# A hybrid attention and linear-attention block: the attention stage issued in the source's order on every engine

## The chip, the cores and the metric

The kernel runs on one core of one Trainium2 chip. A core has a matrix engine (TensorE, PE in the profile), a vector engine (VectorE, DVE), an engine for activation functions and copies (ScalarE, ACT), GpSimd (POOL) and SyncE (SP), which here only issues transfers. Each takes its own instructions in the order in which they were put, and waits for the others through semaphores. The metric is the time of one execution in microseconds of device time (us), the median of a few runs.

## The reference, cut to what matters

One layer on 512 tokens of width 2048, all in float32. A row norm with a scale and a shift gives `h`. One projection of `h` feeds two mixers: 16 heads of attention of width 64, and 4 heads of a gated linear attention (GLA). Both are gated, joined, projected out and added to the input. What the change touches is the attention:

```python
aq, ak, av, ag, gq, gk, gv, gg, lr_f, lr_b = split(h @ w_in)
for window, dilation in ((128, 1), (512, 4), (2048, 16)):
    o_p, lse_p = dilated_window_attention(aq, ak, av, rel_bias, window, dilation)
mix_w = softmax(stack(lses))
att = einsum('pbsh,pbshe->bshe', mix_w, stack(outs))
a_out = att * silu(ag)
```

The kernel computes the three patterns as one softmax per head over all 512 keys: a row of biases for each head holds the relative bias plus the logarithm of how many patterns contain a distance, and a very large penalty where none does.

## The kernel before

**Precision.** TensorE multiplies in a reduced format. So each operand is split into a high part (an ACT copy, for weights `split_hi`, L313) and a low part (a DVE subtraction, `split_lo`, L297), and every product is three matmuls (`three`, L168 to L171).

**Units.** The projections are cut into units of 512 output columns: `qk2`, `qk4`, `qk6` (queries and keys of two pairs of heads each), `gk`, `gv0`, `gv1`, `ag0` to `gg1`, and the output projection. A unit (`unit`, L843) has 8 weight groups of 512 KB. For each group it runs four output tiles, two depth blocks each, three matmuls per block. I call such a block of three matmuls a **tick**: 64 ticks to a unit. The four tiles accumulate in four of five PSUM banks (`PJ`); the unit that follows starts in the bank that is free and then in those of the one before, so these must have been copied out.

**Copying out.** `qk_evict` (L531) copies the queries and keys of a pair out of two banks and splits them. It has four ACT copies of 64 partitions (L539, L548), four DVE subtractions (L540, L550) and four small transfers through SP (L549, L551), which put keys on the other half of the partitions.

**Attention beside the projections.** While one unit multiplies, the attention of the two pairs that the unit before produced runs between its ticks. `attention` (L556) makes 16 tiles (4 heads, 4 blocks of 128 queries), each of these steps:

- `score`: two matmuls (L576, L577) into one of three other banks (`PA`). DVE then adds the bias and takes the row's minimum (L580, here "the reduction"), ACT takes the exponential (L583), DVE the reciprocal of the sum (L584), and POOL scales P (L585).
- `turn`: four TensorE transposes of P into a `PA` bank (L597), a high part by ACT (L601) and a low part by DVE (L602).
- `values`: for two tiles together, eight matmuls into a `PA` bank (L611), an ACT copy (L614) and a DVE addition (L618).

The list `items` says at which share of the unit each step is put (`ATT_AT`, L73). What lies past the unit's end goes into `spill` and is put into the next unit.

**Sums.** Two matrix-vector products (the value bias and the gate of the end) are done by DVE in 48 pieces (`sum_work`, L686), each with a load of 512 KB. `SUMS_IN` (L78) says how many pieces ride in which unit.

**Order.** TensorE's order is that of the source throughout (L145). On the other engines the planner of the first stage sets the order up to L518; from there on a scheduler lists the instructions by their priority, and `urgent` (L837) raises the steps of the attention by 20 places. So an early step of a later unit can come ahead of a late one. All loads of weights go through SP (L286), four buffers deep (`RAW`).

Of the kernel before, what the change touches and what calls it, by code (L numbers as in the profile page):

```python
# [18 lines left out]
P = 128  # L19
# [114 lines left out]
def block_kernel(ctx: ExitStack, tc: tile.TileContext, a: dict):  # L134
# [396 lines left out]
    def qk_evict(p, psq, psk):  # L531

        for j in range(2):
            own = slice(64 * j, 64 * j + 64)
            oth = slice(64 - 64 * j, 128 - 64 * j)
            qs = T2(f"qs{p}{j}", F32R)
            act(qs[own], psq[own, ::-1], AF.Copy, scale=-0.125)  # L539
            stt(qs[oth], psq[own, ::-1], -0.125, qs[own].bitcast(F32),  # L540
                op0=ALU.mult, op1=ALU.subtract)
            stacks[2 * p + j] = [qs, None, None, own]
        for j in range(2):
            own = slice(64 * j, 64 * j + 64)
            oth = slice(64 - 64 * j, 128 - 64 * j)
            ks = T2(f"ks{p}{j}", F32R)
            kl = T2(f"kl{p}{j}", F32R)
            act(ks[own], psk[own], AF.Copy)  # L548
            nc.sync.dma_start(ks[oth].bitcast(F32), ks[own].bitcast(F32))  # L549
            tt(kl[own], psk[own], ks[own].bitcast(F32), op=ALU.subtract)  # L550
            nc.sync.dma_start(kl[oth].bitcast(F32), kl[own].bitcast(F32))  # L551
            stacks[2 * p + j][1:3] = ks, kl

    cat = [None] * 4

    def attention(pairs):  # L556

        tiles = [(2 * p + j, i) for p in pairs for j in range(2) for i in range(4)]
        gt, pt, pr_ = {}, {}, {}
        heads = [2 * p + j for p in pairs for j in range(2)]  # L560

        def g_load(h):
            g = gp.tile([P, 896], F32, tag="g", name=f"g{h}")
            nc.sync.dma_start(g, bass.AP(grow.tensor, grow.offset + h * 1024, [[1, P], [1, 896]]))
            gt[h] = g

        def score(h, i):
            def go():
                if h % 8 == 0 and i == 0:
                    cat[h // 8] = B8(f"cat{h // 8}", [4, 512])  # L570
# [5 lines left out]
                mm(ps, qs[:, q], ks, start=True, stop=False)  # L576
                mm(ps, qs[:, q], kl, start=False, stop=True)  # L577
                t = T2(f"p{h}{i}")
                st = sm.tile([P, 3], F32, tag="st", name=f"st{h}{i}", bufs=6)
                nc.vector.tensor_tensor_reduce(  # L580
                    out=t, in0=ps, in1=gt[h][:, P * i:P * i + 512], op0=ALU.add, op1=ALU.min,
                    scale=1.0, scalar=3e38, accum_out=st[:, 0:1])
                act(t, t, AF.Exp, bias=st[:, 0:1], scale=-1.0, accum_out=st[:, 1:2])  # L583
                nc.vector.reciprocal(st[:, 2:3], st[:, 1:2])  # L584
                nc.gpsimd.tensor_scalar(t, t, st[:, 2:3], 1.0, op0=ALU.mult, op1=ALU.mult)  # L585
                pr_[h, i] = t
            return go

        def turn(h, i):
            def go():  # L590
                half, ii = divmod(i, 2)
                if ii == 0:
                    pt[h, half] = B8(f"pt{h}{half}", [2, 4, 256], F32R)
                t = pr_.pop((h, i))
                pk = PA(f"t{h}{i}")
                for kt in range(4):
                    nc.tensor.transpose(pk[:, kt * P:kt * P + P], t[:, kt * P:kt * P + P], ident)  # L597
                hi = pt[h, half][:, 0, :, P * ii:P * ii + P]
                lo = pt[h, half][:, 1, :, P * ii:P * ii + P]
                src = pk.rearrange("p (k q) -> p k q", k=4)  # L600
                act(hi, src, AF.Copy)  # L601
                tt(lo, src, hi.bitcast(F32), op=ALU.subtract)  # L602
            return go

        def values(h, half):
            def go():
                t = pt.pop((h, half))
                po = PA(f"o{h}{half}")
                for kt in range(4):
# [10 lines left out]

        items = []
        n = len(tiles)
        for x in range(n + 4):
            if x < n:
                items.append(score(*tiles[x]))
            if 2 <= x <= n + 1:
                items.append(turn(*tiles[x - 2]))
            if 3 <= x <= n + 2 and tiles[x - 3][1] % 2 == 1:
                items.append(values(tiles[x - 3][0], tiles[x - 3][1] // 2))
        g_load(heads[0])  # L630
        start, span, move0, move1, move_last = ATT_AT
        at = [start + (q + 0.5) / len(items) * span for q in range(len(items))]
        at[0] -= move0
        at[1] -= move1
        at[-1] += move_last
        return list(zip(at, items))

    def gate_half(m, z):

# [203 lines left out]
    def unit(name, natural, side=(), rhs=None, lr=None, tiles=range(4)):  # L843
# [5 lines left out]
        for q in range(KT // 2):  # L849
            g = gorder[q] if name == "o3" else q  # L850
            i0 = gi[name, g]
            todo = []
            if 0 in tiles:
                todo = list(range(gi[name, gorder[0] if name == "o3" else 0], upto[name, g] + 1))
                for i in todo:
                    split_hi(i)
                for ahead in (1, 2):
                    fetch(upto[name, g] + ahead)
            if i0 not in low:
                split_lo(i0)  # L860
            hi, lo = wts[i0]
            for n, i in enumerate(tiles):
                for kk in range(2):
                    k = 2 * g + kk
                    rh, rl = (h_hi[:, k, :], h_lo[:, k, :]) if rhs is None else rhs[k]
                    if natural:
                        t = slice(i * P, i * P + P)
                        cw = slice(kk * 512, kk * 512 + 512)
                        three(ps[n], rh[:, t], rl[:, t], hi[:, cw], lo[:, cw], q + kk == 0, q + kk == KT // 2)
                    else:  # L870
                        c = slice(kk * 512 + i * P, kk * 512 + i * P + P)
                        three(ps[n], hi[:, c], lo[:, c], rh, rl, q + kk == 0, q + kk == KT // 2)
                    tick += 1
                    if tick % (2 * len(tiles)) == 2:
                        for i_ in todo:
                            split_lo(i_)
                    while pos < len(side) and side[pos][0] * ticks <= tick:
                        urgent(side[pos][1])
                        pos += 1
                if lr is not None:  # L880
                    lr(4 * g + i)
            for i_ in todo:
                split_lo(i_)
        while pos < len(side):
# [12 lines left out]
        lnexp()  # L897


    for p in range(2):  # L900
        qk_evict(p, psb["b", 4 + 2 * p], psb["b", 5 + 2 * p])
    for n, p in (("qk2", 0), ("qk4", 2), ("qk6", 4)):
        ps = unit(n, False, attention((p, p + 1)) + ([(0.05, shift_row)] + some_sums(n) if p == 4 else []))
        for q in range(2):
            qk_evict(p + 2 + q, ps[2 * q], ps[2 * q + 1])

    ps = unit("gk", False, attention((6, 7)) + some_sums("gk"))
    gla["k"] = B8("gkt", [4, 512])
    for i in range(4):
        act(gla["k"][:, i, :], ps[i], AF.Copy)  # L910


    lrb = B8("lrb", [KT, 32])
    nc.sync.dma_start(lrb, a["w_lr"][0])
    lrs = B8("lrs", [KT, 2, 32], F32R)
    act(lrs[:, :, 0, :], lrb, AF.Copy)
    tt(lrs[:, :, 1, :], lrb, lrs[:, :, 0, :].bitcast(F32), op=ALU.subtract)
    plr = PA("plr")

    def lr_tick(n):  # L920
        if n % 2 == 1:
            k = n // 2
            w = lrs[:, k, :, :].rearrange("p a b -> p (a b)")
            mm(plr[:64], w, h_hi[:, k, :], start=k == 0, stop=False)
            mm(plr[:64], w, h_lo[:, k, :], start=False, stop=k == KT - 1)

    ps = unit("gv0", True, some_sums("gv0"), lr=lr_tick)
    gla["v0"] = B8("gv0", [4, 512])
    for i in range(4):
        act(gla["v0"][:, i, :], ps[i], AF.Copy)  # L930
# [200 lines left out]
```

## Time and profile before

| what | us |
|---|---|
| runs: median (lowest to highest of 3) | 962.89 (958.9 to 962.98) |
| the profiled execution, its own time | 959.9 |
| its span, first to last instruction | 957.9 |
| first matmul of `qk2` / `qk4` / `qk6` / `gk` / `gv0` | 191.87 / 257.29 / 323.71 / 390.28 / 457.51 |
| mean granted TensorE clock (1 is full speed) | 0.997 |

The stage that the change orders anew runs from the first matmul of `qk2` to that of `gv1` at 510.39 us. A row of the timeline has start, length, engine, line, operation, output and inputs, count, and in brackets the idle time ahead of it with what ended it. Matmuls overlap: what one costs is the distance from its start to the next start, not its length. "SPq" and "ACTq" are the issues of transfers by these engines.

### The profile page before, as it was taken

To read this page: it belongs to the slowest core of one execution; us is meant where nothing else is said; L and a number is where in the kernel's file an instruction comes from. 1 tells how busy PE (TensorE), PEld (TensorE's weight loads), DVE (VectorE), ACT (ScalarE), POOL (GpSimd) and SP (SyncE) were. 2 spreads that over 40 slices of the span, in tenths; PEclk is the share of its full clock that TensorE was granted. 3 is DMA by queue.
4 is the path that set the end of the run, shared out by engine and by line. 5 is a ranking of instruction groups with operands and counts; after the bars stand their busy time and mean duration, and the time that the engine had idled before them with its cause. 6 is when DMAs were issued, how large, how long until landed. Compare 5 with 4: busy or idle time off the path is not lost.

```text
span 957.9 us, 11999 instructions
## 1 busy us (share of the span) xinstructions
PE 939.7 (98%) x4464; PEld 777.1 (81%) x4464; DVE 605.3 (63%) x900; ACT 431.5 (45%) x719; POOL 81.1 (8%) x100
## 2 busy tenths in 40 slices
PE   8999999999999999999999999999999999999996
PEld 5888788888888888888778888888887888888884
DVE  7988899675756676766435656675964352546421
ACT  5443533565655655655215544543834152233222
POOL 0000000012122022122000000000010000202120
PEclk9999999999999999999999999999999999999998
DMA  9999687443333463533454244354555464244013
GB/s 330 413 411 365 229 296 275 150 131 105 112 103 105 144 200 108 173 127 103 150 176 146 86 132 154 132 176 154 173 195 183 132 221 154 92 151 152 23 55 121
DMA packets 45180, 163.76 MB, mean 171 GB/s; under 512 B 5730, under 2 KB 6018, under 8 KB 40386
## 3 DMA queue, kind: packets, MB, share of 16 engines
q1 hardware_dynamic: 44946, 162.68, 49.9%
q8 instruction: 35, 0.57, 0.2%
q10 hardware_dynamic: 176, 0.33, 0.1%
q14 instruction: 23, 0.18, 0.1%
HBM read 154.51 MB, written 4.28 MB: 166 GB/s over the span
## 4 chain that ended last, share of the span: by engine, by line
PE 84%; DMA 6%; DVE 5%; issue 3%; ACT 1%; SPq 0%; POOL 0%; ACTq 0%; DVEq 0%; POOLq 0%
PE ps_o L170 6%; PE ps_o L169 6%; PE ps_o L171 6%; DMA rawg<-in_wg 6%; PE ps_qk L170 5%; PE ps_qk L169 5%; PE ps_qk L171 5%; PE o L611 3%; PE sta L169 3%; PE sta L170 3%; PE sta L171 3%; PE stb L171 3%; PE stb L169 3%; PE stb L170 3%; PE ps_gv L171 3%; PE ps_gv L170 3%
## 5 line engine op out<-in xcount | busy, mean ns | idle before, releaser
L585 POOL TENSOR_SCALAR p<-p,st 128x512 f32<-128x512 f32 x64 | 45.5, 711 | 406.6 <-DVE st L584 357.9
L244 DVE CUSTOM_DVE_ANT_0 cb<-cb,sb,c_bcond 128x2048 f32<-128x2048 f32 (+1 forms) x32 | 73.4, 2294 | 0.0
L583 ACT ACTIVATE p<-p,st 128x512 f32<-128x512 f32 x64 | 46.1, 721 | 56.8 <-DVE st L580 56.3
L602 DVE TENSOR_TENSOR pt<-t,pt 128x512 fp32r<-128x512 f32 x64 | 44.0, 689 | 16.2 <-ACT pt L601 15.8
L580 DVE CUSTOM_DVE_ANT_0 p<-s,g 128x512 f32<-128x512 f32 x64 | 43.6, 687 | 14.8 <-PE s L577 14.5
L601 ACT ACTIVATE pt<-t 128x512 fp32r<-128x512 f32 x64 | 37.8, 592 | 10.2 <-PE t L597 9.2
L244 DVE CUSTOM_DVE_ANT_0 rawg<-rawg,sb,gate 128x1024 f32<-128x1024 f32 x16 | 20.5, 1283 | 29.6 <-DMA rawg<-in_wg 29.6
L611 PEld LDWEIGHTS o<-pt,vv 128*128 128x128 f32 x256 | 34.7, 188 | 5.0 <-DVE pt L602 2.2
L597 PEld LDWEIGHTS t<-c_ident,p 128*128 128x128 f32 x256 | 31.8, 140 | 8.5
L597 PE MATMUL t<-c_ident,p 128*128 128x128 f32 x256 | 38.3, 272 | 0.0
L611 PE MATMUL o<-pt,vv 128*128 128x256 f32 x256 | 36.6, 283 | 0.9 <-DVE pt L602 0.8
L244 DVE CUSTOM_DVE_ANT_0 rawg<-rawg,sb,c_bcond 128x1024 f32<-128x1024 f32 x16 | 20.5, 1283 | 26.3 <-DMA rawg<-in_wg 26.3
L1014 POOL TENSOR_TENSOR x<-x,fgain 128x512 f32<-128x512 f32 x12 | 20.3, 1696 | 185.3 <-ACT ysq L1012 185.3
L1012 ACT ACTIVATE ysq<-x 128x512 f32<-128x512 f32 x16 | 10.1, 632 | 47.2 <-DVE x L1010 47.2
L767 POOL TENSOR_SCALAR dc<-st,sc 128x256 f32<-128x256 f32 x16 | 10.4, 652 | 245.5 <-DVE st L764 240.6
L1009 DVE TENSOR_TENSOR y<-ps_o,sb 128x512 f32<-128x512 f32 x16 | 10.9, 684 | 25.9 <-PE ps_o L171 25.9
L584 DVE RECIPROCAL st<-st 128x1 f32<-128x1 f32 x64 | 10.3, 162 | 24.9 <-ACT p L583 24.9
L576 PE MATMUL s<-ks,qs 128*128 128x512 f32 x64 | 25.1, 391 | 0.0
L577 PE MATMUL s<-kl,qs 128*128 128x512 f32 x64 | 25.0, 391 | 0.0
L774 ACT ACTIVATE sq<-st,sc 128x256 f32<-128x256 f32 x24 | 12.2, 509 | 26.8 <-DVE st L769 14.3
L1010 DVE TENSOR_TENSOR x<-y,x 128x512 f32<-128x512 f32 x16 | 18.0, 1125 | 0.3
L614 ACT ACTIVATE oh<-o 64x256 f32<-64x256 f32 x32 | 12.2, 382 | 13.0 <-PE o L611 12.2
(1275 smaller groups left out, 2916.7 us busy)
## 6 DMA issues: line engine op xcount, KB each, us to landing
cb<-in_wm SPq DMA_DIRECT2D x31, 1024.0 KB, 7.9
rawg<-in_wg SPq DMA_DIRECT2D x32, 512.0 KB, 3.4
raw_o<-in_w_o SPq DMA_DIRECT2D x32, 512.0 KB, 3.4
raw_qk<-in_w_qk SPq DMA_DIRECT2D x24, 512.0 KB, 3.4
rawb<-in_w_sb SPq DMA_DIRECT2D x16, 512.0 KB, 4.8
rawv<-in_wv SPq DMA_DIRECT2D x16, 512.0 KB, 3.8
raw_gv<-in_w_gv SPq DMA_DIRECT2D x16, 512.0 KB, 3.5
raw_ag<-in_w_ag SPq DMA_DIRECT2D x16, 512.0 KB, 3.3
```

What stands on the lines that cost most here:

```text
L169: mm(ps, lh, rh, start=first, stop=False)
L170: mm(ps, ll, rh, start=False, stop=False)
L171: mm(ps, lh, rl, start=False, stop=last)
L244: nc.vector.tensor_tensor_reduce(out=w, in0=w, in1=with_, op0=ALU.mult, op1=ALU.add, scale=1.0, scalar=init, accum_out=dst)
L576: mm(ps, qs[:, q], ks, start=True, stop=False)
L580: nc.vector.tensor_tensor_reduce(out=t, in0=ps, in1=gt[h][:, P * i:P * i + 512], op0=ALU.add, op1=ALU.min, scale=1.0, scalar=3e38, accum_o ...
L583: act(t, t, AF.Exp, bias=st[:, 0:1], scale=-1.0, accum_out=st[:, 1:2])
L585: nc.gpsimd.tensor_scalar(t, t, st[:, 2:3], 1.0, op0=ALU.mult, op1=ALU.mult)
L597: nc.tensor.transpose(pk[:, kt * P:kt * P + P], t[:, kt * P:kt * P + P], ident)
L601: act(hi, src, AF.Copy)
L602: tt(lo, src, hi.bitcast(F32), op=ALU.subtract)
L611: mm(po[:, :256], vv[h // 4][:, kt, h % 4, :], t[:, w, kt, :], start=kt == 0 and w == 0, stop=kt == 3 and w == 1)
```

## The change

From the copying out of the first pairs to the end of `gv0`, POOL, DVE, ACT and SP now take the source's order too. With it:

- `attention` puts the end of the `score` step (reciprocal and scaling) into a step of its own, `scale`. It lies 0.75 tiles behind the score, and for the last tile ahead of the unit's end. The turn lies 1.8 tiles behind the score, the values 3.2, and a tile takes 0.057 of a unit from a start at 0.12. The last turns and values fall into the next unit.
- `qk_evict` does query and key of one half together.
- The units `qk4`, `qk6` and `gk` begin with a double step: each output tile takes weight groups 0 and 1 before the next tile starts, so the second bank is wanted after 4 ticks instead of 2. The unit ahead splits both groups; the second one's low part comes after its last tick.
- Loads of `qk` and `gk` weights (from the fourth on) and of bias tiles are issued by ACT instead of SP.
- `qk6` and `gk` carry no sums; `gv0` has 12 pieces instead of 9, `gv1` 5 instead of 2, `ag0` 8 instead of 7, `gg1` 5 instead of 4.
- The small weights `lrb` and their splits, wanted in `gv0`, are loaded and split inside `gk`.
- A second way to transpose P (DVE and a trip through memory) is written, but `BY_DVE = ()` leaves it unused: TensorE transposes all of P as before.

```diff
-ATT_AT = (0.17, 0.8, 0.04, 0.05, 0.05)
+ATT_AT = (0.12, 0.057)
+BY_DVE = ()
-SUMS_IN = {"qk6": 4, "gk": 4, "gv0": 9, "gv1": 2, "ag0": 7, "ag1": 9, "gg0": 9}
+SUMS_IN = {"gv0": 12, "gv1": 5, "ag0": 8, "ag1": 9, "gg0": 9}
...
-            nc.sync.dma_start(raws[i], a["w_" + u][g])
+            queue = nc.scalar if u[:2] in ("qk", "gk") and i > 2 else nc.sync
+            queue.dma_start(raws[i], a["w_" + u][g])
...
+            qs, ks, kl = [T2(f"{n}{p}{j}", F32R) for n in ("qs", "ks", "kl")]
             act(qs[own], psq[own, ::-1], AF.Copy, scale=-0.125)
+            act(ks[own], psk[own], AF.Copy)
             stt(qs[oth], psq[own, ::-1], -0.125, qs[own].bitcast(F32),
                 op0=ALU.mult, op1=ALU.subtract)
...
             tt(kl[own], psk[own], ks[own].bitcast(F32), op=ALU.subtract)
-            nc.sync.dma_start(kl[oth].bitcast(F32), kl[own].bitcast(F32))
-            stacks[2 * p + j][1:3] = ks, kl
+            for t in (ks, kl):
+                nc.sync.dma_start(t[oth].bitcast(F32), t[own].bitcast(F32))
+            stacks[2 * p + j] = [qs, ks, kl, own]
...
+        for x in range(n):
+            h, i = tiles[x]
+            items.append((x, score(h, i)))
+            items.append((min(x + 0.75, n - 0.6), scale(h, i)))
+            half, ii = divmod(i, 2)
...
+                items.append((x + 1.8, pe_turn(h, i)))
+                if ii:
+                    items.append((x + 3.2, values(h, half)))
...
+        start, step = ATT_AT
+        return [(start + step * x, go) for x, go in items]
...
+        steps = [order_[:2]] if name in ("qk4", "qk6", "gk") else [order_[:1], order_[1:2]]
+        for step in steps + [[g] for g in order_[2:]]:
             todo = []
             if 0 in tiles:
+                end = upto[name, step[-1]] + (name[:2] == "qk" and step[-1] == order_[-1])
...
+                        if len(step) == 2 and tick == 8:
+                            split_hi(end)
+                            for ahead in (1, 2):
+                                fetch(end + ahead)
+                        if tick == 10 if len(step) == 2 else tick % (2 * len(tiles)) == 2:
+                            for i_ in todo:
+                                if i_ <= upto[name, step[-1]]:
+                                    split_lo(i_)
...
+    with tc.manual_schedule(engines=PLANNED):
+        side = attention((0, 1))
+        for i in range(3):
+            fetch(i)
+        split(0)
+        for p in range(2):
+            qk_evict(p, psb["b", 4 + 2 * p], psb["b", 5 + 2 * p])
+        for n, p in (("qk2", 0), ("qk4", 2), ("qk6", 4)):
+            ps = unit(n, False, side + ([(0.6, shift_row)] if p == 4 else []))
+            side = attention((p + 2, p + 3))
+            for q in range(2):
+                qk_evict(p + 2 + q, ps[2 * q], ps[2 * q + 1])
...
+        ps = unit("gk", False, side + [(0.7, lr_load), (0.85, lambda: lr_part(0)), (0.9, lambda: lr_part(1))])
...
+        ps = unit("gv0", True, some_sums("gv0"), lr=lr_tick)
```

More of the change, by code (lines that the diff above doesn't have):

```diff
@@ L587, in score, with pe_turn @@
             return go
-        def turn(h, i):
+        def pe_turn(h, i):
             def go():
@@ L597, in go @@
                     nc.tensor.transpose(pk[:, kt * P:kt * P + P], t[:, kt * P:kt * P + P], ident)
-                hi = pt[h, half][:, 0, :, P * ii:P * ii + P]
-                lo = pt[h, half][:, 1, :, P * ii:P * ii + P]
+                hi, lo = [pt[h, half][:, e, :, P * ii:P * ii + P] for e in range(2)]
                 src = pk.rearrange("p (k q) -> p k q", k=4)
@@ L622, in attention @@
         n = len(tiles)
[L623 to L629, printed above, removed]
-        g_load(heads[0])
[L631 to L636, printed above, removed]
+        for x in range(n):
+            h, i = tiles[x]
+            items.append((x, score(h, i)))
+            items.append((min(x + 0.75, n - 0.6), scale(h, i)))
+            half, ii = divmod(i, 2)
+            if half in BY_DVE:
+                items.append((x + 1.1, turn(h, i)))
+                items.append((x + 1.5, leave(h, i)))
+                if ii:
+                    for at, piece in zip(BACK_AT, (back, part_hi, part_lo, values)):
+                        items.append((x + at, piece(h, half)))
+            else:
+                items.append((x + 1.8, pe_turn(h, i)))
+                if ii:
+                    items.append((x + 3.2, values(h, half)))
+        items.sort(key=lambda v: v[0])
+        g_load(heads[0])
+        start, step = ATT_AT
+        return [(start + step * x, go) for x, go in items]
     def gate_half(m, z):
@@ L848, in unit @@
         pos, tick, ticks = 0, 0, 16 * len(tiles)
-        for q in range(KT // 2):
-            g = gorder[q] if name == "o3" else q
-            i0 = gi[name, g]
+        order_ = gorder if name == "o3" else list(range(KT // 2))
+        steps = [order_[:2]] if name in ("qk4", "qk6", "gk") else [order_[:1], order_[1:2]]
+        for step in steps + [[g] for g in order_[2:]]:
             todo = []
             if 0 in tiles:
[L854 to L861, printed above, removed]
-            for n, i in enumerate(tiles):
[L863 to L881, printed above, removed]
@@ new lines, in unit @@
+                end = upto[name, step[-1]] + (name[:2] == "qk" and step[-1] == order_[-1])
+                todo = list(range(gi[name, order_[0]], end + 1))
+                if len(step) == 1:
+                    for i in todo:
+                        split_hi(i)
+                    for ahead in (1, 2):
+                        fetch(end + ahead)
+            for g in step:
+                split_lo(gi[name, g])
+            for n, i in enumerate(tiles):
+                for g in step:
+                    hi, lo = wts[gi[name, g]]
+                    for kk in range(2):
+                        k = 2 * g + kk
+                        rh, rl = (h_hi[:, k, :], h_lo[:, k, :]) if rhs is None else rhs[k]
+                        first, last = (g, kk) == (order_[0], 0), (g, kk) == (order_[-1], 1)
+                        if natural:
+                            t = slice(i * P, i * P + P)
+                            cw = slice(kk * 512, kk * 512 + 512)
+                            three(ps[n], rh[:, t], rl[:, t], hi[:, cw], lo[:, cw], first, last)
+                        else:
+                            c = slice(kk * 512 + i * P, kk * 512 + i * P + P)
+                            three(ps[n], hi[:, c], lo[:, c], rh, rl, first, last)
+                        tick += 1
+                        if len(step) == 2 and tick == 8:
+                            split_hi(end)
+                            for ahead in (1, 2):
+                                fetch(end + ahead)
+                        if tick == 10 if len(step) == 2 else tick % (2 * len(tiles)) == 2:
+                            for i_ in todo:
+                                if i_ <= upto[name, step[-1]]:
+                                    split_lo(i_)
+                        while pos < len(side) and side[pos][0] * ticks <= tick:
+                            urgent(side[pos][1])
+                            pos += 1
+                    if lr is not None:
+                        lr(4 * g + i)
@@ L897, in gate_evict @@
         lnexp()
[L900 to L910, printed above, removed]
@@ L913, in block_kernel @@
[L913 to L925, printed above, removed]
```

76 lines of the change are left out of this document (62 added, 14 removed).

## The prediction

> **What bounds the kernel now.** I read the page's summary first, then TensorE's timeline, then what TensorE waits for.
>
> ```profile
> span 957.9 us, 11999 instructions
> ...
> PE 939.7 (98%) x4464; PEld 777.1 (81%) x4464; DVE 605.3 (63%) x900; ACT 431.5 (45%) x719; POOL 81.1 (8%) x100
> ...
> PEclk9999999999999999999999999999999999999998
> ```
>
> TensorE is busy for 98% of the span at full clock, but the lengths of matmuls overlap, so I test it by starts.
>
> ```profile
> 254.54 0.39 PE L171 MATMUL ps_qk<-h_lo,qk27h 128*128 128x512 f32 x1
> 254.77 0.60 PE L597 MATMUL t<-c_ident,p 128*128 128x128 f32 x4
> 255.12 0.48 PE L169 MATMUL ps_qk<-h_hi,qk27h 128*128 128x512 f32 x1
> 255.44 0.40 PE L170 MATMUL ps_qk<-h_hi,qk27l 128*128 128x512 f32 x1
> ...
> 257.29 0.39 PE L169 MATMUL ps_qk<-h_hi,qk40h 128*128 128x512 f32 x1
> 257.52 0.39 PE L170 MATMUL ps_qk<-h_hi,qk40l 128*128 128x512 f32 x1
> 257.74 0.39 PE L171 MATMUL ps_qk<-h_lo,qk40h 128*128 128x512 f32 x1
> 257.97 1.12 PE L611 MATMUL o<-pt,vv 128*128 128x256 f32 x8
> 258.92 0.40 PE L169 MATMUL ps_qk<-h_hi,qk40h 128*128 128x512 f32 x1
> ...
> 263.71 0.39 PE L169 MATMUL ps_qk<-h_hi,qk41h 128*128 128x512 f32 x1
> ...
> 264.39 0.39 PE L576 MATMUL s<-ks,qs 128*128 128x512 f32 x1
> ```
>
> The stream is solid. A wide matmul takes 0.227 us (257.29 to 257.52), a tick 0.68 (263.71 to 264.39), a score's two matmuls 0.45. A turn takes 0.45 (254.54 to 255.44, less two matmuls), the values 0.95 (257.97 to 258.92). The unit `qk4` begins at 257.29 without a gap. What is there to gain is in the waits and around them:
>
> ```profile
> PE o L611 <- DVE pt L602: 0.8, 1, 0.8
> ...
> PE plr L924 <- DVE lrs L917: 0.4, 1, 0.4
> ```
>
> ```profile
> 451.54 0.28 PE L611 MATMUL o<-pt,vv 128*128 128x256 f32 x1
> 452.65 1.10 PE L611 MATMUL o<-pt,vv 128*128 128x256 f32 x7 [0.84 <-DVE pt L602]
> ...
> 461.07 0.39 PE L171 MATMUL ps_gv<-gv00l,h_hi 128*128 128x512 f32 x1
> 461.83 0.42 PE L924 MATMUL plr<-h_hi,lrs 128*64 128x512 f32 x1 [0.38 <-DVE lrs L917]
> ```
>
> By starts these two cost 1.11 - 0.12 = 0.99 and 0.76 - 0.23 = 0.53 us. They are the only waits of TensorE in the view that lie between the first matmul of `qk2` and that of `gv1`. So the ordering can win about 1.5 us and hardly more, and each new wait of TensorE is lost in full.
>
> [...]
>
> **What goes.** The wait at 451.54 goes: in the source's order the values come 1.4 tiles after the turn, 1.4 x 0.057 x 64 = 5.1 ticks or 3.5 us of TensorE and more, and no sums stand ahead of the low part on DVE. The wait for `lrs` goes too, since it is split within `gk`. Sum: -1.5 us.
>
> **What comes: the end of a unit.** I follow DVE in the new order. Durations and latencies come from these rows:
>
> ```profile
> 244.87 0.69 DVE L580 CUSTOM_DVE_ANT_0 p<-s,g 128x512 f32<-128x512 f32 x1
> 245.60 0.72 ACT L583 ACTIVATE p<-p,st 128x512 f32<-128x512 f32 x1 [1.47 <-DVE st L580]
> 246.45 0.16 DVE L584 RECIPROCAL st<-st 128x1 f32<-128x1 f32 x1 [0.88 <-ACT p L583]
> 246.71 0.70 POOL L585 TENSOR_SCALAR p<-p,st 128x512 f32<-128x512 f32 x1 [2.16 <-DVE st L584]
> 246.93 0.69 DVE L602 TENSOR_TENSOR pt<-t,pt 128x512 fp32r<-128x512 f32 x1 [0.32 <-ACT pt L601]
> ...
> 250.10 1.22 DVE L297 TENSOR_TENSOR qk41l<-raw_qk,qk41h 128x1024 fp32r<-128x1024 f32 x1
> 251.24 0.16 DVE L584 RECIPROCAL st<-st 128x1 f32<-128x1 f32 x1
> ...
> 251.56 0.58 ACT L539 ACTIVATE qs<-ps_qk 64x512 fp32r<-64x512 f32 x1
> ...
> 252.42 0.69 DVE L540 SCALAR_TENSOR_TENSOR qs<-ps_qk,qs 64x512 fp32r<-64x512 f32 x1
> 253.13 0.69 DVE L602 TENSOR_TENSOR pt<-t,pt 128x512 fp32r<-128x512 f32 x1
> ...
> 254.58 0.42 DVE L618 TENSOR_TENSOR cat<-o,oh 64x256 f32<-64x256 f32 x1
> ...
> 259.84 0.69 DVE L540 SCALAR_TENSOR_TENSOR qs<-ps_qk,qs 64x512 fp32r<-64x512 f32 x1
> 260.57 0.68 DVE L550 TENSOR_TENSOR kl<-ps_qk,ks 64x512 fp32r<-64x512 f32 x1
> ...
> 261.91 0.69 DVE L550 TENSOR_TENSOR kl<-ps_qk,ks 64x512 fp32r<-64x512 f32 x1 [0.21 <-ACT ks L548]
> ...
> 448.36 0.39 PE L577 MATMUL s<-kl,qs 128*128 128x512 f32 x1
> 448.89 0.69 DVE L580 CUSTOM_DVE_ANT_0 p<-s,g 128x512 f32<-128x512 f32 x1 [1.06 <-PE s L577]
> ```
>
> Now the copying out begins 5.7 us before `qk4` (251.56 against 257.29): the scheduler takes a pair's banks as its tiles finish, and slips the low part of a turn between two copies (253.13). The source's order allows neither. Its order on DVE around the seam is: reduction of tile 15 (score after tick 63), reciprocal (after tick 64), low part of the second weight group (after the last tick), eight operations of `qk_evict`, low part of turn 14 (put at tick 2 of the new unit), addition of values 13, low part of turn 15.
>
> Call T the start of the new unit. The last score's second matmul starts at T - 0.68 - 0.23 = T - 0.91. The reduction starts 0.53 later, the exponential 0.73 after that, the reciprocal 0.85 after that: T + 1.20. With 0.17 for the reciprocal and 1.14 for the weights' low part DVE reaches the copying out at T + 2.51. ACT's first query copy is done by then (it can start at T + 1.1). The eight operations follow at 0.73 (259.84 to 260.57): T + 8.3. The low part of turn 14 ends at T + 9.0.
>
> TensorE meanwhile runs 8 ticks, turns 14 and 15 and values 13, and wants a `PA` bank for the first score at T + 5.44 + 0.90 + 0.95 = T + 7.3. There are three such banks, held by turn 14, values 13 and turn 15, and each is released by a DVE instruction that stands behind the copying out. So TensorE waits 1.7 us. Part of that falls earlier: the second accumulator bank is free after the third of the eight operations, T + 4.7, and wanted at 4 ticks + 0.45 + 0.95 = T + 4.1. The double step hides most of what would be there, not all.
>
> To this comes DVE's own lateness at T. The last step brings it a weight split of 1.14, and its reciprocals wait 0.85 for the exponential each time. Followed by the same durations from tick 47 on, the reduction of tile 15 starts 0.2 us late. I take 1.95 us at each of the three seams (into `qk4`, `qk6`, `gk`): +5.9. Its ends: 1.7 without the lateness, and 1.95 + 0.42 + 0.69 = 3.1 if the first score is given the bank of turn 15 instead of the one that is free first. Into `qk2` nothing spills, and into `gv0` the copies are ACT's alone: nothing there.
>
> **What is hidden.** Inside a unit a turn stands 6.6 ticks behind its score, at least 5.4 us with the work between; the way to a scaled P is 0.3 + 0.73 + 0.85 + 0.26 + 0.70 = 2.8 us and, where a weight split falls between, 2.3 more: enough, by 0.3. Loads issued by ACT cost nothing I can see:
>
> ```profile
> 510.60 0.92 ACTq L946 DMA_DIRECT2D rst<-in_rst  x1
> 510.87 0.58 ACT L930 ACTIVATE gv<-ps_gv 128x512 f32<-128x512 f32 x1
> ```
>
> ACT begins to compute at 510.87 while the issue runs. Were it not hidden, 0.92 for the issue ahead of the copying out adds at most that per seam (in the range). Their buffers were split at least 6 ticks earlier, so the issue itself does not wait. SP keeps the key transfers, and in `gv0` the sums' and weights' loads in turn. [...]
>
> The moved sums are eight pieces of 1.28 us on DVE, three each to `gv0` and `gv1`:
>
> ```profile
> 520.00:540.00 20.00, 20.00 (x93) 16.59 (x92) 14.76 (x19) 11.53 (x23) 0.94 (x2) 1.00 0.38 128
> ```
>
> ```profile
> L244 DVE CUSTOM_DVE_ANT_0 rawv<-rawv,shb,vbias 128x1024 f32<-128x1024 f32 x8 | 10.3, 1282 | 12.0 <-DMA rawv<-in_wv 12.0
> ```
>
> In these 20 us of `gv1` TensorE (the first busy figure) never waits and DVE (the third) is busy for 14.76, so there is room for 3 x 1.28 = 3.8 us over the unit. Without that cover up to 3.8 would be lost. I take 0.
>
> **Sum.** -1.5 + 5.9 = +4.4 us. Against the profiled execution's own 959.9 that is 964.3. The four executions shown (958.9, 959.9, 962.89, 962.98) lie 4 us apart with a mean of 961.2, so I state it on that scale: 961.2 + 4.4, rounded to **966**. Against the median of 962.89 it lies inside 0.5% (958.1 to 967.7), which is about what a measurement of this kernel can tell from no change.
>
> **The rivals.**
>
> *No wait at the seams.* If the new order is not strictly the source's (the spilled turns still go ahead of the copying out), the first score's bank is free in time. Then only -1.5 remains: 958.4 on the profile's scale, 959.7 on the other. For it: today's trace does just this at 253.13. Against it: the change names the engines. Chance 0.2; faster by over 0.5% only by the spread of the runs.
>
> *Clearly slower: DVE is late before the unit ends.* The chain score, exponential, reciprocal, low part is serial in source order, and the last step carries both weight splits on ACT. Taking full lengths (1.22 for a split on DVE, 0.85 for an exponential on ACT) instead of distances between starts, turn 13 waits 1.0 for a bank, the second accumulator bank 2.2 and the first score 1.15: 4.35 per seam, +13 - 1.5 = +11.5, or 972.7. It decides early: against the median my forecast of +4.4 stands only 0.4 us under the bound of 4.8, so 0.15 us of further lateness per seam would carry it over. Chance 0.25, around 972.
>
> *The moved sums hurt GLA.* Up to 3.8 us, on top of the forecast: 970. DVE's 14.76 of 20 us speaks for it, TensorE's 20.00 of 20 against it. Chance 0.05.
>
> **How the numbers follow.** Forecast 0.5 (962 to 970), no wait 0.2, late DVE 0.25, sums 0.05. Of the forecast a third lies above 967.7, of the late case nearly all, of the sums half: slower 0.43. Faster only from the second case: 0.04. Same 0.53. The range leaves out the lower part of "no wait" and the top of "late DVE": 960 to 974.
>
> **What would show it.** In the units `qk4`, `qk6` and `gk`: two gaps of TensorE in the first 10 us, one of 0.5 to 0.8 at the fifth tick, ended by DVE's L540 (its line after the change), and one of about 1.2 before the first score, ended by the low part of a turn. The first copying-out operation of DVE after the unit's first matmul instead of before. No gap at the values near the end of `gk` and none at `plr`. It is wrong if these seams are solid, if gaps lie inside the units (turns that wait for POOL), or if the time is lost after `gv0`.

## The result, and the profile after

| | before | after |
|---|---|---|
| median (lowest to highest, runs), us | 958.43 (956.82 to 962.98, 13) | 965.35 (963.48 to 971.42, 13) |
| the profiled execution, its own time | 959.9 | 965.35 |
| its span | 957.9 | 963.3 |
| start of `qk2` to start of `gv1` | 318.52 | 323.91 |

The changed kernel is slower: the ratio is 1.0073, with a 95% interval of 1.0056 to 1.009. Before has more runs here than the three shown at first, and their median is 4.5 us lower.

The 5.4 us that the span grew are easy to place. I take the length of a unit from its first matmul to that of the next:

| | `qk2` | `qk4` | `qk6` | `gk` | `gv0` | `gv1` | `ag0` | `ag1` | `gg0` |
|---|---|---|---|---|---|---|---|---|---|
| before | 65.42 | 66.42 | 66.57 | 67.23 | 52.88 | 54.17 | 54.14 | 55.42 | 56.56 |
| after | 63.41 | 68.32 | 68.39 | 68.31 | 55.48 | 55.71 | 54.14 | 55.71 | 54.53 |

From `qk2` to `gv0` the sum is +5.39, the start of `qk2` is 0.25 earlier, and all that follows the start of `gv1` comes to +0.3. So the loss lies in the stage that was ordered anew. (`qk2` is shorter and `gv0` longer partly because the last turns and values now fall into the next unit.)

The page's summary of the changed kernel:

```profile
span 963.3 us, 11933 instructions
...
PE 941.2 (98%) x4464; PEld 776.9 (81%) x4464; DVE 601.8 (62%) x901; ACT 429.7 (45%) x720; POOL 82.7 (9%) x100
```

Nothing in it shows the loss: the work is the same and TensorE still reads 98%. The view of what TensorE waits for does (engine, line, what it waited for; total us, times, longest):

```profile
PE s L573 <- DVE pt L606: 2.5, 3, 0.9
PE kt L798 <- DVE ki L788: 1.3, 1, 1.3
...
PE t L602 <- DVE pt L606: 0.6, 1, 0.6
PE ps_qk L174 <- DVE qk61l L302: 0.5, 1, 0.5
PE ps_qk L174 <- DVE qk41l L302: 0.5, 1, 0.5
PE ps_gk L174 <- DVE gk1l L302: 0.5, 1, 0.5
PE ps_gv L173 <- ACT gkt L992: 0.3, 1, 0.3
```

The two waits of before (values at 451.54, `plr` at 461.83) are gone. Two new ones come once at each of the three seams: a weight's low part (`qk41l`, `qk61l`, `gk1l`) and, ahead of the first score, the low part of a turn (`pt`). TensorE's timeline at the seam into `qk4`, which starts at T = 255.03:

```profile
256.41 0.60 PE L602 MATMUL t<-c_ident,p 128*128 128x128 f32 x4
256.76 0.48 PE L173 MATMUL ps_qk<-h_hi,qk41h 128*128 128x512 f32 x1
257.74 0.50 PE L174 MATMUL ps_qk<-h_hi,qk41l 128*128 128x512 f32 x1 [0.50 <-DVE qk41l L302]
...
262.98 0.39 PE L175 MATMUL ps_qk<-h_lo,qk41h 128*128 128x512 f32 x1
264.22 0.50 PE L573 MATMUL s<-ks,qs 128*128 128x512 f32 x1 [0.86 <-DVE pt L606]
```

By starts, with 0.23 for a matmul, the gaps cost 0.98 - 0.23 = 0.75 and 1.24 - 0.23 = 1.01. The other two seams read the same within 0.01. DVE's timeline at the same place shows one unbroken queue:

```profile
254.82 0.68 DVE L577 CUSTOM_DVE_ANT_0 p<-s,g 128x512 f32<-128x512 f32 x1
...
256.40 0.16 DVE L588 RECIPROCAL st<-st 128x1 f32<-128x1 f32 x1 [0.88 <-ACT p L580]
256.48 1.20 DVE L302 TENSOR_TENSOR qk41l<-raw_qk,qk41h 128x1024 fp32r<-128x1024 f32 x1
257.71 0.69 DVE L546 SCALAR_TENSOR_TENSOR qs<-ps_qk,qs 64x512 fp32r<-64x512 f32 x1
...
262.75 0.69 DVE L548 TENSOR_TENSOR kl<-ps_qk,ks 64x512 fp32r<-64x512 f32 x1
263.48 0.69 DVE L606 TENSOR_TENSOR pt<-t,pt 128x512 fp32r<-128x512 f32 x1
```

The weight's low part waits in it for the reciprocal, and that for the exponential. The low part of turn 14 stands behind eight operations of copying out: it ends at 264.17, T + 9.1, and TensorE's score starts 0.05 later.

### The profile page after: what moved, and what is told of

Its sections match the earlier page's. It is cut to its first block, busy times and chain, and to the rows that moved or that the text cites. A ratio compares the mean times of both kernels' runs of the same rounds, so it can differ in the third digit from the quotient of the medians.

```text
span 963.3 us, 11933 instructions
## 1 busy us (share of the span) xinstructions
PE 941.2 (98%) x4464; PEld 776.9 (81%) x4464; DVE 601.8 (62%) x901; ACT 429.7 (45%) x720; POOL 82.7 (9%) x100
## 5 line engine op out<-in xcount | busy, mean ns | idle before, releaser
L666 DVE TENSOR_TENSOR cat<-o,oh 64x256 f32<-64x256 f32 x32 | 13.4, 418 | 37.3 <-ACT oh L662 37.1
L573 PE MATMUL s<-ks,qs 128*128 128x512 f32 x64 | 27.2, 424 | 2.5 <-DVE pt L606 2.5
```

## The experiments

All kernels ran against the kernel before on the same chip; its median was 958.3 to 958.5 each time. Theory A: the order of DVE's queue at the seams makes the loss. Rivals: ACT's new loads, the double step, the moved sums, or a lack of room that only moves from one waiting instruction to another.

### 1. The order alone

```diff
-    with tc.manual_schedule(engines=PLANNED):
+    with ExitStack():
```

> The fixed source order of POOL, DVE, ACT and SP is taken off again from the attention stage; all other parts of the change stay. Theory A: the order alone makes the waits at the seams; without it the three seams are solid (5.3 us less) and the wait at gv0 shrinks (about 1 less): 959 to 961. Rival (the double step, the spilled turns or the loads by ACT make the waits): they stay, 964 to 966.

958.94 us (956.61 to 960.78, 11 runs), ratio 0.9999 (0.9984 to 1.0013). With the scheduler's order `qk4`, `qk6`, `gk` and `gv0` last 66.29, 66.40, 66.28 and 54.14, and from `qk2` to `gv1` it is 316.75: 1.77 less than before, 7.16 less than after. So the source's order alone costs 7.16 us in this stage, 2.0 at each of the three seams (68.32 against 66.29) and 1.35 in `gv0` (55.48 against 54.13). This run frees all four engines at once. That DVE's order is the one that counts at the three seams is read from the rows; no run frees it alone. DVE's timeline of this kernel shows what the scheduler does otherwise (`qk4` starts at 255.79):

```profile
256.14 0.68 DVE L546 SCALAR_TENSOR_TENSOR qs<-ps_qk,qs 64x512 fp32r<-64x512 f32 x1
256.85 0.68 DVE L548 TENSOR_TENSOR kl<-ps_qk,ks 64x512 fp32r<-64x512 f32 x1
257.46 0.15 DVE L588 RECIPROCAL st<-st 128x1 f32<-128x1 f32 x1
257.63 0.69 DVE L546 SCALAR_TENSOR_TENSOR qs<-ps_qk,qs 64x512 fp32r<-64x512 f32 x1
258.36 0.69 DVE L548 TENSOR_TENSOR kl<-ps_qk,ks 64x512 fp32r<-64x512 f32 x1
259.08 0.69 DVE L606 TENSOR_TENSOR pt<-t,pt 128x512 fp32r<-128x512 f32 x1
```

It begins to copy out while the last exponential runs, puts the reciprocal between two copies, and takes the low part of turn 14 after four copies instead of eight: it is done at T + 4.0, not T + 9.1. What this wins is given back in `gv1`, which lasts 56.04:

```profile
PE kt L798 <- DVE ki L788: 1.7, 1, 1.7
```

### 2. The weight's low part earlier

```diff
-                                if i_ <= upto[name, step[-1]]:
-                                    split_lo(i_)
+                                split_lo(i_)
```

> The low part of the second weight group of the next unit goes back to tick 58, beside that of the first group, instead of after the unit's last tick. Theory A (one chain on DVE from the last score to the low part of turn 14 sets both waits at a seam): the 1.14 us only move along the chain. The wait for that low part (0.75 by starts, three times) goes, but the reduction of tile 15 comes about 1 us later and the wait before the first score grows from 1.0 to about 2. Total per seam 1.8 to 2.1 as against 1.76, time 965 to 966.5. Theory B (each wait is its own): the first wait goes, the second stays at 1.0, 2.2 us less, about 963.

966.09 us (964.05 to 969.24, 6 runs), ratio 1.0081 (1.006 to 1.0102). The seam costs as much (units 68.28, 68.50, 68.01). DVE begins to copy only 0.3 us earlier, at T + 2.4: it now waits 0.32 us for ACT's first copy, which stands behind the last exponential. TensorE's rows at the seam into `qk4`:

```profile
261.15 0.50 PE L173 MATMUL ps_qk<-h_hi,qk40h 128*128 128x512 f32 x1 [0.26 <-DVE qs L546]
...
265.48 0.51 PE L573 MATMUL s<-ks,qs 128*128 128x512 f32 x1 [0.84 <-DVE pt L606]
```

The first wait is now for the second accumulator bank, the one that the prediction had expected. The weight's low part had only hidden it. The time is that of theory A in the expectation, its picture is not quite: by starts the two gaps are 0.43 and 1.01, so the score's wait did not grow.

### 3. The first score later

```diff
-ATT_AT = (0.12, 0.057)
+ATT_AT = (0.155, 0.0545)
```

> The attention of a unit starts at 0.155 instead of 0.12 with a pace of 0.0545 instead of 0.057, so the first score of a unit stands after tick 10 instead of tick 8 and the last steps stay where they were to within a tick. Theory A: two ticks more, 1.36 us, cover the wait of 1.0 for the score's bank at the three seams; the wait for the weights' low part (0.75) stays. 3 us less, about 962.3. Rival (the bank of turn 15 is what the score gets, or the denser pace brings waits inside the units): the second wait shrinks by less, or new ones come: 964 or more.

964.64 us (963.39 to 965.45, 5 runs), ratio 1.0063 (1.0044 to 1.0083): 0.7 under the changed kernel, and not the expected saving of 3; the rival's time came out. The weight's low part still makes its gap. No score waits any more, but the next consumer of the same chain does, the values of the last two tiles:

```profile
PE o L659 <- DVE pt L606: 1.6, 3, 0.5
```

### 4. The loads back on SP

```diff
-            queue = nc.scalar if u[:2] in ("qk", "gk") and i > 2 else nc.sync
+            queue = nc.sync
...
-            nc.scalar.dma_start(g, bass.AP(grow.tensor, grow.offset + h * 1024, [[1, P], [1, 896]]))
+            nc.sync.dma_start(g, bass.AP(grow.tensor, grow.offset + h * 1024, [[1, P], [1, 896]]))
```

> The loads of qk and gk weights and of bias tiles go back from ACT to SP, in source order. Theory A: nothing, 965.3 within 1. Rival (issues by ACT hold up its copies at the seams): up to 0.9 us less per seam, about 963. If SP now holds loads behind the key transfers, a weight group comes late: more than 966.

965.4 us (964.27 to 966.58, 5 runs), ratio 1.0075 (1.0053 to 1.0097), with the same waits at the seams. The issues by ACT cost nothing and win nothing here: 965.4 with these loads on SP against 965.35 with them on ACT.

### 5. Without the double step

```diff
-        steps = [order_[:2]] if name in ("qk4", "qk6", "gk") else [order_[:1], order_[1:2]]
+        steps = [order_[:1], order_[1:2]]
```

> The double step at the start of qk4, qk6 and gk is taken away; the order stays. Theory A: the second accumulator bank is wanted after 2 ticks, about 1.8 us into the unit, and DVE releases it at 4.8: a wait of 3.0 per seam at the third tick, which then covers the two others. 3 x (3.0 - 1.76) = 3.7 us more, about 969. If the double step hides nothing: 965.3.

973.51 us (971.63 to 975.33, 4 runs), ratio 1.0155 (1.0142 to 1.0169). The two waits become one, for the second accumulator bank at the third tick:

```profile
PE ps_qk L173 <- DVE qs L546: 5.8, 2, 2.9
...
PE ps_gk L173 <- DVE qs L546: 2.9, 1, 2.9
```

By starts it is 3.0 each time: the copying out alone decides when a bank comes free, and the double step hides part of it. But the units last 71.01, 69.58 and 70.99. Against 66.3 to 66.4 of the listed order, `qk6` loses the wait and little else, 3.2, while `qk4` and `gk` lose 4.7. That is told at the end. It makes up about what the expectation missed in the profiled execution, whose span is 969.7 against 963.3: 3.7 of these 6.3 were expected. The median is higher yet, 8.2 over the changed kernel's.

### 6. The copying out of the first pair ahead of the unit's end

With the edit of run 2, and:

```diff
+            early = [(0.926 + 0.05 * j, lambda p=p, j=j: qk_evict(p + 2, now[0], now[1], (j,))) for j in range(2)]
+            ps = unit(n, False, side + early + ([(0.6, shift_row)] if p == 4 else []))
...
-            for q in range(2):
-                qk_evict(p + 2 + q, ps[2 * q], ps[2 * q + 1])
+            qk_evict(p + 3, ps[2], ps[3])
```

> Still the source's order. The first pair's copying out is taken apart and put into the unit that produces it, one half behind the score of tile 14, one behind that of tile 15, where DVE now waits for exponentials; the low part of the second weight group goes to tick 58. The second pair stays where it was. Theory A (DVE's chain behind the last score sets all waits at a seam): four of the eight operations (2.9 us) and the split (1.14) leave the chain, more than the 1.76 us of waits; the three seams are solid, 5.3 us less, about 960; the wait at gv0 (1.2) and the one in gv1 stay. Rival (the order has further waits behind these, as the later first score showed): the waits only move, 963 or more.

965.41 us (964.82 to 967.99, 5 runs), ratio 1.0081 (1.0068 to 1.0094). My expectation fell. The waits for DVE at the seams are gone, but turns 14 and 15 now wait for POOL at every seam, because the reciprocals stand behind the copies (units 68.42, 68.52 and 68.07):

```profile
PE t L602 <- POOL p L589: 3.0, 6, 0.6
```

### 7. The copying out of the second pair behind the turns

With the edit of run 2, queries of both halves ahead of the keys, and:

```diff
-            for q in range(2):
-                qk_evict(p + 2 + q, ps[2 * q], ps[2 * q + 1])
+            qk_evict(p + 2, ps[0], ps[1])
+            side.append((0.08, lambda p=p, ps=ps: qk_evict(p + 3, ps[2], ps[3])))
```

> The changed kernel, still in the source's order on every engine: the low part of the second weight group goes with the first, and the copying out of a unit's second pair goes behind the low parts of turns 14 and 15. Theory A, the eight copying-out operations and the weight's low part in one queue ahead of the turn's low part are the whole of the seam: VectorE begins to copy at T+1.4, frees the second accumulator bank at T+2.9 (wanted T+4.1), turn 14's bank at T+5.0 (wanted T+7.3); all seams are solid, units qk4, qk6 and gk last 66.3 to 66.6, the time is 965.35 - 5.3 = 960.0. Rival, as in the run with the copying out ahead of the unit's end, the waits only move: to the banks of the second pair (the fourth tile, wanted at T+9.5) or to a score that waits for the keys of the second pair; over 1 us at each seam and a time above 963.5.

969.38 us (968.77 to 970.86, 4 runs), ratio 1.0118 (1.0104 to 1.0131): worse than the change. The time is again that of the rival, but the wait stands at neither of the places that the rival named. The first scores find their banks; it is the turn of the first tile that waits for POOL, 1.5 us at each seam (and 0.6 once in `qk2`):

```profile
PE t L605 <- POOL p L592: 5.1, 4, 1.5
```

DVE's timeline at the seam into `qk4` tells why:

```profile
266.54 0.69 DVE L546 SCALAR_TENSOR_TENSOR qs<-ps_qk,qs 64x512 fp32r<-64x512 f32 x1 [0.72 <-ACT qs L545]
267.26 0.68 DVE L552 TENSOR_TENSOR kl<-ps_qk,ks 64x512 fp32r<-64x512 f32 x1
268.67 0.69 DVE L552 TENSOR_TENSOR kl<-ps_qk,ks 64x512 fp32r<-64x512 f32 x1 [0.72 <-ACT ks L551]
269.39 0.69 DVE L580 CUSTOM_DVE_ANT_0 p<-s,g 128x512 f32<-128x512 f32 x1
```

DVE reaches the copying out at T + 2.4 here too, not T + 1.4. The first score's bank is free in time, but the reduction, possible 0.53 after the first score's second matmul at 264.74, starts only at 269.39, behind the second pair. And my order by queries and keys made it worse: a DVE operation follows its own ACT copy directly, and waits 0.66 to 0.72 for it four times. So this run doesn't say what the same place would cost with ACT ahead.

### 8. The sums

The sums of the changed kernel in the kernel before, then the attention stage in the scheduler's order with 2 pieces in `gv1` as before, then no piece in `gv1` (one of its five goes to `ag0`, four to `gg1`) with the source's order and with the scheduler's. `ki` are the decayed keys of the linear attention, made by DVE, and `kt` their transposes on TensorE:

```diff
-SUMS_IN = {"qk6": 4, "gk": 4, "gv0": 9, "gv1": 2, "ag0": 7, "ag1": 9, "gg0": 9}
+SUMS_IN = {"qk6": 0, "gk": 0, "gv0": 12, "gv1": 5, "ag0": 8, "ag1": 9, "gg0": 9}
...
-SUMS_IN = {"gv0": 12, "gv1": 5, "ag0": 8, "ag1": 9, "gg0": 9}
+SUMS_IN = {"gv0": 15, "gv1": 2, "ag0": 8, "ag1": 9, "gg0": 9}
...
-SUMS_IN = {"gv0": 12, "gv1": 5, "ag0": 8, "ag1": 9, "gg0": 9}
+SUMS_IN = {"gv0": 12, "gv1": 0, "ag0": 9, "ag1": 9, "gg0": 9}
```

> The kernel before with the change's distribution of the sums alone (none in qk6 and gk, 12 in gv0, 5 in gv1, 8 in ag0). Theory: the wait for the low part of a turn at the end of gk goes (1.0 less), and the wait for GLA's decayed keys in gv1 comes (1.5 to 1.9 more, as with the order taken off): 958.5 to 959.5. Rival (the wait in gv1 comes from the rest of the change): 957 to 957.5.

> The change without the fixed order, and with 15 sums in gv0 and 2 in gv1, as many in gv1 as before. Theory: the wait for the decayed keys in gv1 (1.7 us) goes and what the attention stage won (1.8 us from qk2 to gv1) is left: 956.5 to 957.5, faster than both. Rival (the wait has another cause than the three more sums in gv1, or 15 sums bring loads of weights late in gv0): 958.5 or more.

> The changed kernel with no sums in gv1 (gv0 12, gv1 0, ag0 9, ag1 9, gg0 9, gg1 9). Theory C, the pieces that stand in VectorE's queue ahead of the gates of gv1 make the wait of the kt transposes: the wait of 1.3 us is gone, gv1 lasts 54.2 instead of 55.7, the three seams keep their 0.75 + 1.01 each, the time is 1.5 below the changed kernel's 965.35: 963.9. Rival, the wait comes from the lists of the later units as they begin after the attention stage, whatever sums are in gv1: kt still waits 1.3 us and the time stays at 965.4.

> The changed program with the scheduler's order and no sums in gv1. Theory C: the attention stage stays 1.8 us shorter than before, the kt wait of 1.7 us is gone, so the time is 958.9 - 1.7 = 957.2, 1.2 below the kernel before. Rival, the scheduler puts another piece or another split into the same chain: kt still waits and the time stays at 958.9.

| | median, us | ratio (95%) | `gv1` | `kt` waits |
|---|---|---|---|---|
| before with the new sums | 960.74 | 1.0029 (1.0017 to 1.0041) | 55.56 | 1.2 |
| listed, 15 in `gv0`, 2 in `gv1` | 959.19 | 1.0005 (0.9993 to 1.0017) | 56.14 | 1.3 + 0.3 |
| source's order, none in `gv1` | 965.0 | 1.0067 (1.0053 to 1.0081) | 54.17 | no |
| listed, none in `gv1` | 957.25 | 0.9984 (0.9971 to 0.9996) | 54.15 | no |

With no piece in `gv1` the wait of `kt` goes in both orders, and `gv1` lasts what it lasted before. Two pieces were enough to make it in one kernel and not in the kernel before, so their number isn't the cause. What counts is whether a piece stands ahead of the chain that ends in `ki`, and when its load lands. In the changed kernel:

```profile
526.23 0.75 DVE L765 TENSOR_SCALAR g<-z,c_gbias 128x512 f32<-128x512 f32 x1 [1.50 <-ACT e L761]
527.94 1.23 DVE L733 CUSTOM_DVE_ANT_0 rawv<-rawv,shb 128x1024 f32<-128x1024 f32 x1 [0.97 <-DMA rawv<-in_wv]
...
535.52 1.28 DVE L248 CUSTOM_DVE_ANT_0 rawv<-rawv,shb,vbias 128x1024 f32<-128x1024 f32 x1
...
541.13 1.23 DVE L302 TENSOR_TENSOR gv16l<-raw_gv,gv16h 128x1024 fp32r<-128x1024 f32 x1 [0.60 <-ACT gv16h L318]
542.27 0.68 DVE L788 TENSOR_TENSOR ki<-ki,gkt 128x512 f32<-128x512 f32 x1
```

The piece at 527.94 holds DVE for 0.97 us of waiting for its load and 1.2 of work, in the middle of the gates of the first head, and another stands ahead of their second half; a weight's low part (541.13), which came behind `ki` in the kernel before, now stands ahead of it. `ki` starts 26.7 us into the unit instead of 23.2: 1.5 us of this come at the first piece, 1.1 at the second, 0.9 at the weight. The transposes `kt` then wait 1.31 us for `ki`. In the listed kernel with two pieces it is a single piece, of which the kernel before has the like in the same place (its row comes last):

```profile
522.75 1.28 DVE L248 CUSTOM_DVE_ANT_0 rawg<-rawg,sb,c_bcond 128x1024 f32<-128x1024 f32 x1 [3.94 <-DMA rawg<-in_wg]
...
523.96 0.75 DVE L765 TENSOR_SCALAR g<-z,c_gbias 128x512 f32<-128x512 f32 x1
```

```profile
519.92 1.29 DVE L244 CUSTOM_DVE_ANT_0 rawg<-rawg,sb,c_bcond 128x1024 f32<-128x1024 f32 x1 [1.73 <-DMA rawg<-in_wg]
```

The first gate follows a piece that waited 3.94 us for its load, and comes 15.1 us after the unit's start (508.84) instead of 10.7 as in the kernel before, where the piece waited 1.73. SP issued that load 8.7 us into the unit (517.58) instead of 6.1 (516.50).

The last kernel is the fastest of all: 1.2 us under before, and its interval excludes 1, just. It keeps the other edits of the change but for the sums, and drops its order. The third wins 1.7 us from `gv1` to `gg0` by the units (218.39 against 220.09), but 0.35 by the medians, with overlapping intervals. Its profile begins `qk2` 1.34 us later than the changed kernel's; scatter of that size hides the gain, and the times don't settle it.

The kernel before with the new sums holds one more answer. The wait of the values at the end of `gk` was still there, though no piece rides in `gk`:

```profile
PE o L611 <- DVE pt L602: 0.8, 1, 0.8
```

### 9. All repairs together

The source's order of run 7, no piece in `gv1`, and the first two copies of `gk`'s results ahead of the unit's end:

```diff
+        side += [(0.95, lambda: gk_copy(0)), (0.98, lambda: gk_copy(1))]
...
-        for i in range(4):
-            act(gla["k"][:, i, :], ps[i], AF.Copy)
+        for i in range(2, 4):
+            gk_copy(i)
```

> As the run before, and no sums in gv1, and the first two copies of gk's results issued by ScalarE before the unit's end, where it is idle for 1.4 us. If the four places (three seams, the seam into gv0, the chain in gv1) are all that the change costs, the time is 965.35 - 5.3 - 1.2 - 1.5 = 957.4, about 1 us under the kernel before (958.4). Rival: what is won is given back in later units, as where the sums now ride in ag0 and gg1, and the time is 959 or more.

968.17 us (966.67 to 968.71, 4 runs), ratio 1.0098 (1.0082 to 1.0114). `gv1` lasts 54.17, but the seams keep run 7's waits, turn 15 in `gv0` now waits 1.3 instead of 0.75, and `ag0` loses 3.8 us to 57.93, though the kernel of run 8 with the same pieces there lasts 54.55. DVE's and TensorE's rows show where:

```profile
610.42 1.28 DVE L248 CUSTOM_DVE_ANT_0 rawg<-rawg,sb,c_bcond 128x1024 f32<-128x1024 f32 x1 [3.90 <-DMA rawg<-in_wg]
```

```profile
613.22 0.46 PE L861 MATMUL go<-at,gv 128*128 128x128 f32 x2 [1.89 <-DVE at L847]
```

Again a piece waits for its load ahead of a chain, here the one that ends in `at`, and the matmuls `go` wait for `at`: 2.05 us by starts. Then TensorE ran at half clock from 614.55 to 617.97, which takes another 1.7, half of 3.42 (see the last section). In the kernel of run 8 the same piece waited 2.19 us, and `go` 0.2. The expectation fell. No source order that I wrote beats the scheduler's; that there is none isn't shown.

## Why the prediction was right or wrong

**The time.** 966.0 was forecast, 965.35 measured, inside the range. But the forecast called "within 0.5%" likeliest, and the change is slower by 0.73%, its interval wholly above 0.5%. The step that failed is the scale: four executions with a mean of 961.2 stood for the kernel before, and over 13 runs its median is 958.43. The nearness of 966.0 to 965.35 owes much to chance: the base was 2.8 too high and the change's own cost too low, +4.4 against +5.4 in the profiled executions and +6.9 by the medians.

**What goes: -1.5.** Both waits went. The listed kernel, with all edits but the order and with solid seams, is 1.77 shorter. One reason was half wrong: "no sums stand ahead of the low part on DVE" had nothing to do with it, as the wait stayed when the sums left `gk`. What is left of the step is the larger distance between turn and values; no run changes that alone.

**The seams: +5.9.** Right in mechanism and size: 1.95 forecast, 1.76 in two gaps, 2.0 by the units' lengths against the listed order. DVE's chain came out row by row: copying out from T + 2.68 (forecast T + 2.51 and 0.2 of lateness), low part of turn 14 done at T + 9.1 (forecast T + 9.0 and 0.2). The first of the two gaps was put down to the second accumulator bank; it was the second weight group's low part, at the third tick and not the fifth, which stood in the very list of the forecast and whose own consumer I had not looked for. With that out of the way (run 2) the bank made a gap of the same kind. Without the double step the same chain cost 3.0 each time, as it had to.

**The seam into `gv0`: "nothing there".** Wrong, 1.2 us in gaps (1.35 by the unit): 0.44 while TensorE waits for the first of ACT's copies itself, 0.75 ahead of turn 15. Two timelines of the changed kernel, ACT's and then DVE's:

```profile
461.69 2.04 ACT L992 ACTIVATE gkt<-ps_gk 128x512 f32<-128x512 f32 x4
463.60 1.08 ACT L318 ACTIVATE gv01h<-raw_gv 128x1024 fp32r<-128x1024 f32 x1
```

```profile
464.71 1.23 DVE L302 TENSOR_TENSOR gv01l<-raw_gv,gv01h 128x1024 fp32r<-128x1024 f32 x1 [2.73 <-ACT gv01h L318]
465.85 0.68 DVE L606 TENSOR_TENSOR pt<-t,pt 128x512 fp32r<-128x512 f32 x1
```

That the copies are ACT's alone was true. But a weight's high part stands behind them on ACT, its low part waits 2.73 us for it on DVE, and turn 14's low part waits behind that. A stall crossed from one queue into another. The forecast had followed only DVE's own work.

**The moved sums: 0.** Wrong in place: `gv1` grew by 1.54, and none of it is there when no sums ride in it. 14.76 busy us of 20 were read as room; but part of DVE's 5 us of rest were waits inside a chain (0.53 and twice 0.80 us for ACT, on the way to `ki`), and a piece that waited 0.97 us for its load in front of the chain made `ki` 1.5 us later. It was half a rival ("up to 3.8", 0.05). In the profile after `gg0` was 2.03 shorter, which makes up for it in the sum of the units; why it was shorter isn't shown. The same sums cost the kernel before 0.29%.

**The loads by ACT: 0.** Right: the sum has no term for them, and run 4 measured 965.4 us with them on SP against 965.35 on ACT.

**The rivals.** The scheduler's slipping of the turns, which "no wait at the seams" hoped for, is just what the listed kernel shows and the source's order forbids. "DVE is late" had 4.35 per seam; the lateness that it added didn't come.

## What to carry to other kernels

When an order becomes fixed, write out each engine's queue around a seam, and for every entry ask who waits for it, the weights' splits too; then follow a stall through the next engine's queue, since that is where the seam into `gv0` was lost. A busy share of 74% (14.76 of 20 us in `gv1`) on an engine that ran a serial chain was no room: a piece that waited for its own load in front of the chain delayed all of it (0.97 us of waiting and 1.2 of work, `ki` 1.5 us later). And where a queue was simply full for 7.7 us (256.48 to 264.17), moving one consumer moved the wait, as in runs 2, 3, 6 and 7. As I read its rows, the listed order won because it mixed both streams finely, not because any one piece was early; no run separates the two.

## What the runs showed of the hardware

The kernel without the double step has three waits of 2.9 us. After those into `qk4` and `gk` TensorE came back at full clock and then fell to half for 3.41 us; after the one into `qk6` it didn't. The stretches around the wait into `qk4` (the first two rows) and at the end of the one into `qk6` (the last), each with the busy times of PE, PEld, DVE, ACT and POOL and then the granted clock:

```profile
258.17:261.58 3.41, 1.06 (x6) 0.93 (x7) 3.25 (x6) 2.25 (x4) 0.70 (x1) 1.00 0.49 123
```

```profile
261.58:264.99 3.41, 3.41 (x14) 2.93 (x13) 3.25 (x6) 2.16 (x4) 0.00 (x0) 0.50 0.87 191
```

```profile
329.85:333.26 3.41, 1.73 (x11) 1.59 (x12) 3.25 (x6) 2.50 (x5) 0.03 (x1) 1.00 0.54 128
```

In the matmuls of that kernel:

```profile
260.52 0.50 PE L173 MATMUL ps_qk<-h_hi,qk40h 128*128 128x512 f32 x1 [2.88 <-DVE qs L546]
...
262.81 0.63 PE L173 MATMUL ps_qk<-h_hi,qk40h 128*128 128x512 f32 x1
263.24 0.63 PE L174 MATMUL ps_qk<-h_hi,qk40l 128*128 128x512 f32 x1
```

The distance between starts is 0.43 (262.81 to 263.24) instead of 0.23, and the unit costs 1.4 us more than `qk6` (71.01 against 69.58). Behind the wait into `gk` the granted clock read 0.50 from 402.20 to 404.70; behind the one into `qk6` it read 1.00 from 332.30 to 336.00. In run 9 half clock followed a wait of 1.89 us in `ag0`, from 614.55 to 617.97. After the waits of 0.86 us into `qk4` and of 1.31 us in `gv1` in the changed kernel the granted clock stayed 1.00 (264.20 to 268.00, 543.01 to 547.00).

Why three waits of 2.9 us ended unlike isn't shown: no run moves such a wait and leaves the rest as it was.
